# Wide matrix products as two half-width f32 products in place of three f32r products

## The chip, the cores and the metric

The kernel runs on one core of one Trainium2 chip. The metric is the device time of one execution in microseconds (us), lower is better. TensorE (PE) multiplies matrices, VectorE (DVE) and ScalarE (ACT) do elementwise work, GpSimd (POOL) a few odd jobs, and SyncE (SP) issues most transfers. PEld is TensorE's loading of the stationary operand, which the profile lists apart from the products (PE).

## The reference, cut to what matters

The reference is a two-layer decoder over 1024 tokens of width 1024 in float32. Each layer norms its input, projects it, mixes (pooling in layer 0, sliding-window attention in layer 1, and attention to 256 memory tokens in both), projects back, and then runs a squared-ReLU MLP of width 4096. All large products are float32 products:

```python
proj = rmsnorm(h, norm_mix[l]) @ w_in[l]
...
mkv = rmsnorm(mem, mem_norm[l]) @ w_mem_kv[l]
...
s = jnp.einsum('bshd,bmhd->bhsm', q, mk).astype(jnp.float32) * (HEAD_DIM ** -0.5)
...
h = h + jnp.concatenate([main_out, mem_out], axis=-1) @ w_out[l]
h = h + sq_relu_mlp(rmsnorm(h, norm_mlp[l]), w_up[l], w_down[l])
```

## The kernel before, in words

Features lie on the 128 partitions and tokens on the free axis, in two halves of 512. A wide product takes a stationary operand of 128x128 (weights) and a moving operand of 128x512 (activations) and adds into one PSUM bank. To keep float32 precision with the faster rounded type float32r, both operands are split: ACT writes a rounded copy, "hi", and DVE writes the remainder, "lo", which is the source minus hi. A product is then three float32r products, hi by hi, hi by lo, and lo by hi. This triple stands in four places of the code: `mm3` (lines 270 to 272; projections, memory keys, pooling, output projection of layer 1), `scores` (lines 515 to 517; attention scores), `Stream.run` (lines 938, 940 and 941; both MLPs and the output projection of layer 0, by a seven-product block scheme) and `plain_unit` (lines 1035 to 1037; the first step of each MLP). By the program, 2456 triples have 512 moving columns (1848 in `Stream.run`, 476 in `mm3`, 68 in `scores`, 64 in `plain_unit`) and 82 have 256.

Some other products are plain float32 already: transposes (`transpose4`, line 277, 128 columns), sums over heads or rows (lines 544, 313), and the attention's products with the values. These last have 64 output partitions each and come in twos, one for partitions 0 to 63 and one for 64 to 127: line 601 (128 columns, 128 products) in the memory attention, line 1484 (384 columns, 60 products) in the sliding window.

The splits are made in `split` (lines 233 to 237), `split_hi` and `split_lo` (lines 651 and 654), `stack_keys` (line 481) and a few places by hand. Weights come by DMA on SP's queue; the split MLP inputs are stored in DRAM once and fetched again for later blocks (`win`, 512 KB a transfer, hi and lo).

Order of the work: instructions of an engine run in the order in which they are written out. In the MLPs, `Stream` places each split, sum and eviction at a unit of four triples by due times and by the estimated load of DVE and ACT. In the attention stages, generators (`mem_attn`, `swa`, `head_stats`) are advanced by `tick(us)`, which is called with 0.65 after each triple; a generator's `yield 3.61` means that its next part is written out after triples worth 3.61 us. So the argument of `tick` sets how many wide products stand between two parts of the attention.

Of the kernel before, what the change touches and what calls it, by code (L numbers as in the profile page):

```python
# [10 lines left out]
F32R = mybir.dt.float32r  # L11
# [6 lines left out]
P = 128  # L18
# [23 lines left out]
def kernel(  # L42
# [25 lines left out]

# [44 lines left out]

    def x_tile(shape=None, dtype=F32R):
        return xp.tile(shape or [P, 2, HALF], dtype, tag="x", name="x")
# [113 lines left out]
    def split(src, dst, gain=None):  # L229

        hi, lo = dst[:, 0], dst[:, 1]
        if gain is None:
            nc.scalar.activation(hi, src, AF.Copy)
            nc.vector.tensor_tensor(lo, src, hi.bitcast(F32), op=ALU.subtract)  # L234
        else:
            nc.scalar.activation(hi, src, AF.Copy, scale=gain)
            nc.vector.scalar_tensor_tensor(lo, src, gain, hi.bitcast(F32), op0=ALU.mult, op1=ALU.subtract)
# [11 lines left out]
    def split_unit(raw, nk, gain=None):  # L249
        parts = []  # L250
        for k0 in range(0, nk, 4):
            n = min(4, nk - k0)
            r = raw[:, k0:k0 + n, :]
            if gain is not None:
                nc.gpsimd.tensor_tensor(  # L255
                    r, r, gain[:, k0:k0 + n].rearrange("p (k o) -> p k o", o=1).broadcast_to([P, n, P]), op=ALU.mult)
            w = wp.tile([P, 2, 4, P], F32R, tag="w", name="w")
# [6 lines left out]
    def mm3(ps, wsel, asel, ks, us=0.65):  # L264

        n = len(ks)
        for i, k in enumerate(ks):
            w0, w1 = wsel(k, 0), wsel(k, 1)
            a0, a1 = asel(k, 0), asel(k, 1)
# [71 lines left out]
    def load_x(nrm, between):  # L341
        for n in range(NK):
            h[n] = h_tile()
        xsum = small(NT, "xsum")
        toks = []
        load_gains()
        for t in range(NT):
            xt = g_tile()
            nc.sync.dma_start(out=xt, in_=x2[t * P:(t + 1) * P, :])
            toks.append(xt)  # L350
            if t == 1:
                between()
            if t == 7:
                load_vectors()
        def half(hf):
            tk = toks[4 * hf:4 * hf + 4]
            if hf == 0:
                banks = [tr_tile(), tr_tile(), mm_tile(), mm_tile(), mm_tile(), sps_tile(), sps_tile(), pv_tile().rearrange("p a t -> p (a t)")]
                for j in range(4):
                    for n in range(NK):  # L360
                        nc.tensor.transpose(banks[n][:, j * P:(j + 1) * P], tk[j][:, n * P:(n + 1) * P], ident)
            for n in range(NK):
                if hf == 0:
                    ps = banks[n]
# [10 lines left out]
                eng = nc.gpsimd if n % 3 == 1 else nc.vector  # L375
                eng.tensor_tensor(m[:, 1], h[n][:, hs(hf)], m[:, 0].bitcast(F32), op=ALU.subtract)
# [12 lines left out]
        return half, finish  # L389
# [29 lines left out]
    def mem_layer(l, alloc):  # L419
# [5 lines left out]
        for kk in range(4):  # L425
            m = alloc([P, 2, 2, MEMLEN], F32R)
# [37 lines left out]
        for u in range(4):  # L464
            wsel = load_unit([(ALL, w_mem_kv[l][:, u * P:(u + 1) * P])], NK)
            ps = mm_tile()[:, 0:MEMLEN]
            mm3(ps, wsel, asel, range(NK), 0.33)
# [7 lines left out]
    def stack_keys(src, hi, lo):  # L475


        for e in range(2):
            ln = slice(64 * e, 64 * e + 64)
            nc.scalar.activation(hi[e][ln], src[ln], AF.Copy)  # L480
            nc.vector.tensor_tensor(lo[e][ln], src[ln], hi[e][ln].bitcast(F32), op=ALU.subtract)

    def clear_other(t):

        for e in range(2):
            nc.gpsimd.memset(t[64 - 64 * e:P - 64 * e, :, e, :].bitcast(F32), 0.0)

    def mem_keys(kv):
        hi = z.mkp.tile([P, 2, 2, MEMLEN], F32R, tag="mkh", name="mkh")
        lo = z.mkp.tile([P, 2, 2, MEMLEN], F32R, tag="mkl", name="mkl")  # L490
        clear_other(hi)
        clear_other(lo)
        for j in range(2):
            stack_keys(kv[:, j * MEMLEN:(j + 1) * MEMLEN], [hi[:, j, e, :] for e in range(2)],
                       [lo[:, j, e, :] for e in range(2)])
        return hi, lo
# [3 lines left out]
    def query_stack(key, chunks, n):  # L500

        if n % 2 == 0:
            c = slice(n * P, n * P + 2 * P)
            out_ = []
            for q in chunks:
                st = z.qsp.tile([P, 2, 2 * P], F32R, tag="qs", name="qs")
# [5 lines left out]
    def scores(ps, st, n, khi, klo):  # L512
# [50 lines left out]
    def mem_attn(key, n, mk, vt, mq, rm, od):  # L563
# [4 lines left out]
        khi, klo = mk  # L568
# [3 lines left out]
        for j in range(2):  # L572
# [3 lines left out]
            scores(s_ps, qs[j], n, khi[:, j], klo[:, j])  # L576
# [76 lines left out]
    def split_lo(src, dst):  # L653
        nc.vector.tensor_tensor(dst[:, 1], src, dst[:, 0].bitcast(F32), op=ALU.subtract)  # L654
# [19 lines left out]
    class Stream:  # L674
# [16 lines left out]
        def stationary(self):  # L691

            turn[0] += 1
            return wp.tile([P, 2, 4, P], F32R, tag="w", name="w") if turn[0] % 5 else g_tile([P, 2, 4, P], F32R)
# [25 lines left out]
        def split_pieces(self, due, src, make, pre, x=0, w=0):  # L720
# [13 lines left out]
            b = self.piece(due, lambda: split_lo(src(), box[0]), dve=LO, pre=[a])  # L734
            return a, b, box

        def add_block(self, wt, b, fin, evac, pairs=range(4), cached=None, store=None, alloc=x_tile, b_in_x=False,
# [9 lines left out]
            for j, m in enumerate(ORDER):  # L747
# [7 lines left out]
                if cached:  # L755
                    for c in range(4):
                        def fetch(c=c, step=step, m=m):
                            t = step.win[c] = alloc([P, 2, HALF], F32R)
                            nc.sync.dma_start(out=t.bitcast(F32), in_=cached[m][c])
# [3 lines left out]
                else:  # L763
                    self.sums(m, b, fin, T, wins, first)
                    n, t = {1: (0, 0), 2: (1, 0), 3: (1, 1), 4: (0, 0), 5: (None, None), 6: (0, 0), 7: (0, 1)}[m]
                    for c in range(4):
# [8 lines left out]
                        def make(step=step, c=c):  # L775
                            step.win[c] = alloc([P, 2, HALF], F32R)
# [5 lines left out]
                        if store:  # L782
                            self.piece(first + 1, lambda m=m, c=c, step=step: nc.sync.dma_start(
                                out=store[m][c], in_=step.win[c].bitcast(F32)), pre=[lo], gap=1)
# [122 lines left out]
        def run(self, plain=()):  # L907
# [5 lines left out]
            for i in range(-len(plain), n):  # L913
# [22 lines left out]
                for k in range(4):  # L936
                    x_ = step.win[k]
                    nc.tensor.matmul(ps, w[:, 0, k, :], x_[:, 0], start=m in (1, 2, 7) and k == 0, stop=False,  # L938
                                     skip_group_check=True)
                    nc.tensor.matmul(ps, w[:, 0, k, :], x_[:, 1], start=False, stop=False, skip_group_check=True)  # L940
                    nc.tensor.matmul(ps, w[:, 1, k, :], x_[:, 0], start=False, stop=k == 3, skip_group_check=True)  # L941
                    tick(0.65)
# [40 lines left out]
    def mlp(l, nrm, gain, wt0, ws, hook, then=None):  # L983
        store = {m: [dr.tile([P, 2, HALF], F32, name=f"win{l}_{m}_{c}") for c in range(4)] for m in ORDER}
# [41 lines left out]
        def plain_unit(hf, q):  # L1026
            work = []
            for k in (2 * q, 2 * q + 1):
                for n in range(2):
                    def mm(k=k, n=n):  # L1030
# [4 lines left out]
                        nc.tensor.matmul(ps, w[:, 0, k % 4, :], x_[:, 0], start=k == 0, stop=False)  # L1035
                        nc.tensor.matmul(ps, w[:, 0, k % 4, :], x_[:, 1], start=False, stop=False)
                        nc.tensor.matmul(ps, w[:, 1, k % 4, :], x_[:, 0], start=False, stop=k == NK - 1)
# [164 lines left out]
    def pool_diff(c, hf, u, levels):  # L1202
# [16 lines left out]
        if (c, hf) == (1, 1):  # L1219
            d = z.dp.tile([P, 2, HALF], F32R, tag="d", name="d")  # L1220
        else:
            d = (g_tile if c else h_tile)([P, 2, HALF], F32R)
        d_t[hf][c] = d
        for (a, b, wi) in parts:
# [9 lines left out]
            nc.vector.tensor_tensor(d[a:b, 1], df[a:b, :], d[a:b, 0].bitcast(F32), op=ALU.subtract)  # L1234
# [115 lines left out]
    def head_unit(weights, gain, kgain, dst):  # L1350
# [3 lines left out]
        def tail(hf, ps):  # L1354
# [11 lines left out]
            else:  # L1366
                nc.vector.scalar_tensor_tensor(y, y, kgain, bp, op0=ALU.mult, op1=ALU.mult)
                yk = y.rearrange("p (b k) -> p b k", k=P)
                stack_keys(yk, [dst[hf][:, :, e, :] for e in range(2)], [dst[2 + hf][:, :, e, :] for e in range(2)])
# [29 lines left out]
    def k_unit(pr, alloc):  # L1399
        kh[pr] = [(alloc if i < 3 else g_tile)([P, 4, 2, P], F32R) for i in range(4)]  # L1400
# [15 lines left out]
    def swa(n, pr, put):  # L1416
# [15 lines left out]
        for i in range(3):  # L1432
# [3 lines left out]
            if first_ // 4 == last_ // 4:  # L1436
                kb = slice(first_ % 4, last_ % 4 + 1)
                scores(s_ps[:, 2 - nb:, :, :], qs[i], n, kh[pr][n // 4][:, kb], kh[pr][2 + n // 4][:, kb])
            else:
                for b, k in ((0, first_), (1, last_)):  # L1440
                    scores(s_ps[:, b, :, :], qs[i], n, kh[pr][k // 4][:, k % 4], kh[pr][2 + k // 4][:, k % 4])
# [160 lines left out]
```

## Time and profile before

| | |
|---|---|
| time, median of 2 runs | 1921.91 us (1920.87 to 1922.95) |
| profiled execution: time, span | 1920.99 us, 1919.3 us |
| granted TensorE clock, mean | 0.997 |
| PE busy | 1875.7 us (98%) |
| PEld busy | 1519.3 us (79%) |
| DVE busy | 1416.0 us (74%) |
| ACT busy | 985.9 us (51%) |

An engine's busy time is the time in which at least one of its instructions runs; products overlap in the records, so the distance from one start to the next is a product's price, not its own duration. A row of a timeline has the start and the length of a run of equal instructions and, in brackets, what ended the engine's idle time before it.

### The profile page before, as it was taken

To read this page: it belongs to the slowest core of one execution; us is meant where nothing else is said; L and a number is where in the kernel's file an instruction comes from. 1 tells how busy PE (TensorE), PEld (TensorE's weight loads), DVE (VectorE), ACT (ScalarE), POOL (GpSimd) and SP (SyncE) were. 2 spreads that over 40 slices of the span, in tenths; PEclk is the share of its full clock that TensorE was granted. 3 is DMA by queue.
4 is the path that set the end of the run, shared out by engine and by line. 5 is a ranking of instruction groups with operands and counts; after the bars stand their busy time and mean duration, and the time that the engine had idled before them with its cause. 6 is when DMAs were issued, how large, how long until landed. Compare 5 with 4: busy or idle time off the path is not lost. (4 is left out here: it accounts for less than half of the span.)

```text
span 1919.3 us, 24542 instructions
## 1 busy us (share of the span) xinstructions
PE 1875.7 (98%) x8786; PEld 1519.3 (79%) x8786; DVE 1416.0 (74%) x2577; ACT 985.9 (51%) x2063; POOL 197.4 (10%) x244
## 2 busy tenths in 40 slices
PE   8999999999999999999999999999999999999999
PEld 6867878878888888888768776787888888888887
DVE  6788899896496497489673668679885596496495
ACT  7553654843553553555453666555643643543553
POOL 4502120000000000001424221140000000000000
PEclk9999999999999999999999999999999999999999
DMA  6311423617307407411211123234546227307412
GB/s 253 110 28 52 175 78 142 263 70 278 135 23 285 154 24 262 175 55 67 88 39 39 28 73 97 62 104 197 198 161 226 96 90 262 132 24 284 153 45 66
DMA packets 139052, 244.44 MB, mean 127 GB/s; under 512 B 20852, under 2 KB 67762, under 8 KB 138930
## 3 DMA queue, kind: packets, MB, share of 16 engines
q1 hardware_dynamic: 137458, 238.15, 35.6%
q10 hardware_dynamic: 1472, 4.73, 0.6%
q8 instruction: 69, 1.13, 0.2%
q14 instruction: 53, 0.43, 0.1%
HBM read 196.71 MB, written 46.14 MB: 127 GB/s over the span
## 5 line engine op out<-in xcount | busy, mean ns | idle before, releaser
L651 ACT ACTIVATE w<-wa 128x512 fp32r<-128x512 f32 x371 | 230.9, 624 | 216.4 <-PE mm L941 99.5
L654 DVE TENSOR_TENSOR w<-wa,w 128x512 fp32r<-128x512 f32 x371 | 255.2, 688 | 100.0 <-ACT w L651 99.9
L941 PE MATMUL mm<-x,w 128*128 128x512 f32 x676 | 263.4, 390 | 1.1 <-DVE w L654 1.1
L938 PE MATMUL mm<-x,w 128*128 128x512 f32 x676 | 263.5, 390 | 0.2 <-DVE h L974 0.2
L940 PE MATMUL mm<-x,w 128*128 128x512 f32 x676 | 263.1, 389 | 0.0
L270 PE MATMUL mm<-x,w 128*128 128x512 f32 x448 | 183.4, 411 | 3.9 <-DVE h L374 2.1
L938 PE MATMUL sps<-x,w 128*128 128x512 f32 x468 | 182.8, 391 | 2.3 <-ACT x L651 2.3
L966 DVE TENSOR_TENSOR wa<-wa 128x512 f32<-128x512 f32 x264 | 181.0, 693 | 5.3 <-DMA wa<-in_w_up 4.6
L941 PE MATMUL sps<-x,w 128*128 128x512 f32 x468 | 182.5, 390 | 1.0 <-DVE w L654 1.0
L940 PE MATMUL sps<-x,w 128*128 128x512 f32 x468 | 182.1, 389 | 0.0
L272 PE MATMUL mm<-x,w 128*128 128x512 f32 x448 | 178.0, 398 | 1.0 <-DVE w L234 0.9
L271 PE MATMUL mm<-x,w 128*128 128x512 f32 x448 | 178.4, 399 | 0.4 <-DVE x L234 0.4
L941 PEld LDWEIGHTS mm<-x,w 128*128 128x128 f32 x676 | 126.9, 188 | 28.7 <-DVE w L654 2.2
L938 PEld LDWEIGHTS mm<-x,w 128*128 128x128 f32 x676 | 126.9, 188 | 26.8 <-issue 0.6
L940 PEld LDWEIGHTS mm<-x,w 128*128 128x128 f32 x676 | 126.9, 188 | 26.3
L651 ACT ACTIVATE x<-g 128x512 fp32r<-128x512 f32 x192 | 115.4, 620 | 54.9 <-DVE g L966 54.9
L654 DVE TENSOR_TENSOR x<-g,x 128x512 fp32r<-128x512 f32 x192 | 132.1, 688 | 9.1 <-ACT x L651 9.1
L974 DVE TENSOR_TENSOR h<-mm,h 128x512 f32<-128x512 f32 x124 | 85.0, 685 | 38.4 <-PE mm L941 38.4
L255 POOL TENSOR_TENSOR raw<-raw,cols 128x512 f32<-128x512 f32 x40 | 47.1, 1197 | 639.5 <-DMA raw<-in_w_in 597.5
L997 ACT ACTIVATE g<-g 128x512 f32<-128x512 f32 x90 | 56.9, 632 | 103.9 <-DVE g L1016 103.9
L270 PEld LDWEIGHTS mm<-x,w 128*128 128x128 f32 x448 | 85.0, 190 | 26.2 <-issue 5.3
L938 PEld LDWEIGHTS sps<-x,w 128*128 128x128 f32 x468 | 87.9, 188 | 21.4 <-ACT x L651 3.1
(353 smaller groups left out, 4035.5 us busy)
## 6 DMA issues: line engine op xcount, KB each, us to landing
x<-win SPq DMA_DIRECT2D x168, 512.0 KB, 6.1
wa<-in_w_up SPq DMA_DIRECT2D x32, 1024.0 KB, 5.8
wa<-in_w_down SPq DMA_DIRECT2D x32, 1024.0 KB, 5.1
win<-x SPq DMA_DIRECT2D x56, 512.0 KB, 3.0
h<-hd SPq DMA_DIRECT2D x16, 512.0 KB, 3.6
raw<-in_w_in SPq DMA_DIRECT2D x10, 512.0 KB, 3.8
g<-in_x SPq DMA_DIRECT2D x8, 512.0 KB, 6.7
raw<-in_w_mem_kv SPq DMA_DIRECT2D x8, 512.0 KB, 3.7
```

What stands on the lines that cost most here:

```text
L255: nc.gpsimd.tensor_tensor(r, r, gain[:, k0:k0 + n].rearrange("p (k o) -> p k o", o=1).broadcast_to([P, n, P]), op=ALU.mult)
L270: nc.tensor.matmul(ps, w0, a0, start=i == 0, stop=False)
L271: nc.tensor.matmul(ps, w0, a1, start=False, stop=False)
L272: nc.tensor.matmul(ps, w1, a0, start=False, stop=i == n - 1)
L651: nc.scalar.activation(dst[:, 0], src, AF.Copy)
L654: nc.vector.tensor_tensor(dst[:, 1], src, dst[:, 0].bitcast(F32), op=ALU.subtract)
L938: nc.tensor.matmul(ps, w[:, 0, k, :], x_[:, 0], start=m in (1, 2, 7) and k == 0, stop=False, skip_group_check=True)
L940: nc.tensor.matmul(ps, w[:, 0, k, :], x_[:, 1], start=False, stop=False, skip_group_check=True)
L941: nc.tensor.matmul(ps, w[:, 1, k, :], x_[:, 0], start=False, stop=k == 3, skip_group_check=True)
L966: eng.tensor_tensor(out_, a, b, op=op)
L974: nc.vector.tensor_tensor(c, ps, c, op=ALU.add)
L997: nc.scalar.activation(c, c if src is None else src, AF.Relu)
```

## The change

Operands stay float32: hi is a plain float32 copy that ACT makes, and no remainder is made. A wide product is two plain float32 products with the same moving operand, one of stationary columns 0 to 63 into PSUM partitions 0 to 63, one of columns 64 to 127 into partitions 64 to 127. `tick` gets 0.43 in place of 0.65 (0.22 in place of 0.33 at 256 columns). Operand tiles and the `win` transfers have half the bytes.

```diff
 def split(src, dst, gain=None):
-        hi, lo = dst[:, 0], dst[:, 1]
         if gain is None:
-            nc.scalar.activation(hi, src, AF.Copy)
-            nc.vector.tensor_tensor(lo, src, hi.bitcast(F32), op=ALU.subtract)
+            nc.scalar.activation(dst[:, 0], src, AF.Copy)
...
-    def mm3(ps, wsel, asel, ks, us=0.65):
+    def pair(ps, w, a, start, stop, **kw):
+        for e in (slice(0, 64), slice(64, P)):
+            nc.tensor.matmul(ps[e], w[:, e], a, start=start, stop=stop, **kw)
+
+    def mm3(ps, wsel, asel, ks, us=0.43):
...
-            nc.tensor.matmul(ps, w0, a0, start=i == 0, stop=False)
-            nc.tensor.matmul(ps, w0, a1, start=False, stop=False)
-            nc.tensor.matmul(ps, w1, a0, start=False, stop=i == n - 1)
+            w0, a0 = wsel(k, 0), asel(k, 0)
+            pair(ps, w0, a0, i == 0, i == n - 1)
             tick(us)
...
     def scores(ps, st, n, khi):
-        nc.tensor.matmul(ps, st[:, 0, t], khi, start=True, stop=False)
-        nc.tensor.matmul(ps, st[:, 0, t], klo, start=False, stop=False)
-        nc.tensor.matmul(ps, st[:, 1, t], khi, start=False, stop=True)
+        pair(ps, st[:, 0, t], khi, True, True)
...
     def split_lo(src, dst):
-        nc.vector.tensor_tensor(dst[:, 1], src, dst[:, 0].bitcast(F32), op=ALU.subtract)
+        pass
...
             for k in range(4):
                     x_ = step.win[k]
-                    nc.tensor.matmul(ps, w[:, 0, k, :], x_[:, 0], start=m in (1, 2, 7) and k == 0, stop=False,
-                                     skip_group_check=True)
-                    nc.tensor.matmul(ps, w[:, 0, k, :], x_[:, 1], start=False, stop=False, skip_group_check=True)
-                    nc.tensor.matmul(ps, w[:, 1, k, :], x_[:, 0], start=False, stop=k == 3, skip_group_check=True)
-                    tick(0.65)
+                    pair(ps, w[:, 0, k, :], x_[:, 0], m in (1, 2, 7) and k == 0, k == 3, skip_group_check=True)
+                    tick(0.43)
```

PE's order in the memory attention of layer 0, before: transposes of the weights `s`, products with the values (`pv<-pt,mkv`) and wide products of the projection (`mm<-x,w`) alternate.

```order
L277 MATMUL tr<-ident,s 128x128 x8
L270 MATMUL mm<-x,w 128x512
L271 MATMUL mm<-x,w 128x512
L272 MATMUL mm<-x,w 128x512
...
L601 MATMUL pv<-pt,mkv 64x128
L271 MATMUL mm<-x,w 128x512
L277 MATMUL tr<-ident,s 128x128 x4
L601 MATMUL pv<-pt,mkv 64x128 x3
```

The same place after the change (line 261 is the product in `pair`, 273 the transpose, 587 the product with the values):

```order
L273 MATMUL tr<-ident,s 128x128 x8
L261 MATMUL mm<-x,w 64x512 x4
L273 MATMUL tr<-ident,s 128x128 x4
L261 MATMUL mm<-x,w 64x512
L273 MATMUL tr<-ident,s 128x128 x4
L261 MATMUL mm<-x,w 64x512
L587 MATMUL pv<-pt,mkv 64x128 x8
```

The products with the values now stand together, wide products of 64 output partitions stand alone between transposes of 128, and a pair can be cut in two by them. Over the whole program PE's order goes from half-width to full-width products and back 113 times, 59 times before.

DVE's order in the first MLP, before (lines 654 are the remainders, 966 sums, 974 evictions):

```order
L654 TENSOR_TENSOR x<-g,x 128x512
L654 TENSOR_TENSOR w<-wa,w 128x512
L966 TENSOR_TENSOR wa<-wa 128x4x128
L974 TENSOR_TENSOR h<-sps,h 128x512
L654 TENSOR_TENSOR w<-wa,w 128x512
L654 TENSOR_TENSOR x<-g,x 128x512
```

After the change (sums are line 949, evictions 957):

```order
L949 TENSOR_TENSOR wa<-wa 128x4x128
L949 TENSOR_TENSOR g<-g 128x1024
L957 TENSOR_TENSOR h<-pv,h 128x512
L949 TENSOR_TENSOR wa<-wa 128x4x128
L957 TENSOR_TENSOR h<-sps,h 128x512
```

The remainders are gone from DVE's order and nothing takes their place there.

## Rows read from the trace of the kernel before

**Rows 1.** The page: span, busy time of the engines, granted clock in 40 slices.
```profile
span 1919.3 us, 24542 instructions
PE 1875.7 (98%) x8786; PEld 1519.3 (79%) x8786; DVE 1416.0 (74%) x2577; ACT 985.9 (51%) x2063; POOL 197.4 (10%) x244
PEclk9999999999999999999999999999999999999999
```

**Rows 2.** What PE waited for: total us, times, longest; longest in total first.
```profile
PE mm L361 <- POOL t L163: 4.3, 1, 4.3
PE sps L515 <- ACT s L582: 3.8, 4, 1.5
PE tr L277 <- DVE t L1360: 2.4, 2, 1.8
...
PE mm L361 <- DMA g<-in_x: 0.4, 1, 0.4
```

**Rows 3.** Line 940, window 500 to 800 us: duration min/median/max, first and last start.
```profile
L940 PE MATMUL mm<-x,w x179: 389/389/389, 500.0 to 792.4; 128*128 128x512 f32 x179
L940 PE MATMUL sps<-x,w x116: 389/389/389, 504.8 to 797.9; 128*128 128x512 f32 x116
L940 PE MATMUL pv<-x,w x59: 389/389/389, 510.2 to 799.9; 128*128 128x512 f32 x59
L940 PE MATMUL mm<-x,g x40: 389/389/389, 502.1 to 776.1; 128*128 128x512 f32 x40
L940 PE MATMUL sps<-x,g x32: 389/389/389, 556.5 to 762.5; 128*128 128x512 f32 x32
L940 PE MATMUL pv<-x,g x16: 389/389/389, 570.1 to 789.7; 128*128 128x512 f32 x16
```

**Rows 4.** PE's timeline, triples of 512 columns beside the attention.
```profile
1143.09 0.39 PE L271 MATMUL mm<-x,w 128*128 128x512 f32 x1
1143.32 0.40 PE L272 MATMUL mm<-x,w 128*128 128x512 f32 x1
1143.55 0.40 PE L270 MATMUL mm<-x,w 128*128 128x512 f32 x1
...
1144.01 0.40 PE L272 MATMUL mm<-x,w 128*128 128x512 f32 x1
```

**Rows 5.** PE's timeline, a triple of 256 columns in the memory layer.
```profile
54.01 0.28 PE L271 MATMUL mm<-g,w 128*128 128x256 f32 x1
...
54.37 0.28 PE L271 MATMUL mm<-g,w 128*128 128x256 f32 x1
```

**Rows 6.** Line 1484: all records of its products and loads on one of its tiles.
```profile
L1484 PEld LDWEIGHTS pv<-pt,g x88: 132/137/137, 1074.2 to 1245.3; 128*64 128x64 f32 x88
L1484 PE MATMUL pv<-pt,g x88: 486/486/537, 1074.5 to 1245.6; 128*64 128x384 f32 x88
L1484 PE MATMUL pv<-pt,h x32: 486/512/537, 1073.8 to 1152.9; 128*64 128x384 f32 x32
```

**Rows 7.** PE's timeline, two products of line 1484, then two more.
```profile
1152.57 0.87 PE L1484 MATMUL pv<-pt,h 128*64 128x384 f32 x4
1153.26 0.81 PE L1484 MATMUL pv<-pt,g 128*64 128x384 f32 x4
```

**Rows 8.** PE's timeline, line 1484 alone and in twos, between full-width products.
```profile
1175.66 0.27 PE L277 MATMUL tr<-ident,s 128*128 128x128 f32 x1
1175.86 0.86 PE L1484 MATMUL pv<-pt,g 128*64 128x384 f32 x2
1176.65 0.50 PE L270 MATMUL mm<-x,w 128*128 128x512 f32 x1
1177.08 0.87 PE L1484 MATMUL pv<-pt,g 128*64 128x384 f32 x4
```

**Rows 9.** Line 601: all its records (as rows 6), then eight products on PE's timeline.
```profile
L601 PE MATMUL pv<-pt,mkv x256: 272/273/324, 97.6 to 1014.8; 128*64 128x128 f32 x128
...
1011.53 1.09 PE L601 MATMUL pv<-pt,mkv 128*64 128x128 f32 x16
```

**Rows 10.** PEld's timeline, the loads for the products of rows 7.
```profile
1152.57 0.20 PEld L1484 LDWEIGHTS pv<-pt,h 128*64 128x64 f32 x4
1152.94 0.14 PEld L1484 LDWEIGHTS pv<-pt,g 128*64 128x64 f32 x2 [0.18 <-issue]
```

**Rows 11.** The page: the largest remainder groups on DVE, the rounded copies on ACT.
```profile
L651 ACT ACTIVATE w<-wa 128x512 fp32r<-128x512 f32 x371 | 230.9, 624 | 216.4 <-PE mm L941 99.5
L654 DVE TENSOR_TENSOR w<-wa,w 128x512 fp32r<-128x512 f32 x371 | 255.2, 688 | 100.0 <-ACT w L651 99.9
L654 DVE TENSOR_TENSOR x<-g,x 128x512 fp32r<-128x512 f32 x192 | 132.1, 688 | 9.1 <-ACT x L651 9.1
```

**Rows 12.** The page: the largest group of transfers, KB each and us to landing.
```profile
x<-win SPq DMA_DIRECT2D x168, 512.0 KB, 6.1
```

More of the change, by code (lines that the diff above doesn't have):

```diff
@@ L112, in g_tile, with x_tile @@
         return gp.tile(shape or [P, S], dtype, tag="g", name="g")
-    def x_tile(shape=None, dtype=F32R):
-        return xp.tile(shape or [P, 2, HALF], dtype, tag="x", name="x")
+    def x_tile(shape=None, dtype=F32):
+        return xp.tile(shape or [P, 1, HALF], dtype, tag="x", name="x")
     def t_tile(shape=None):
@@ L229, in split @@
     def split(src, dst, gain=None):
-        hi, lo = dst[:, 0], dst[:, 1]
         if gain is None:
-            nc.scalar.activation(hi, src, AF.Copy)
-            nc.vector.tensor_tensor(lo, src, hi.bitcast(F32), op=ALU.subtract)
-        else:
-            nc.scalar.activation(hi, src, AF.Copy, scale=gain)
-            nc.vector.scalar_tensor_tensor(lo, src, gain, hi.bitcast(F32), op0=ALU.mult, op1=ALU.subtract)
+            nc.scalar.activation(dst[:, 0], src, AF.Copy)
+        else:
+            nc.scalar.activation(dst[:, 0], src, AF.Copy, scale=gain)
     def fetch_unit(srcs, nk):
@@ L425, in mem_layer @@
         for kk in range(4):
-            m = alloc([P, 2, 2, MEMLEN], F32R)
+            m = alloc([P, 1, 2, MEMLEN], F32)
             for i in range(2):
@@ L466, in mem_layer @@
             ps = mm_tile()[:, 0:MEMLEN]
-            mm3(ps, wsel, asel, range(NK), 0.33)
+            mm3(ps, wsel, asel, range(NK), 0.22)
             y = y_tile([P, MEMLEN])
@@ L473, in mem_layer, with stack_keys @@
         return kv, vt
-    def stack_keys(src, hi, lo):
+    def stack_keys(src, hi):
         for e in range(2):
@@ L480, in stack_keys @@
             nc.scalar.activation(hi[e][ln], src[ln], AF.Copy)
-            nc.vector.tensor_tensor(lo[e][ln], src[ln], hi[e][ln].bitcast(F32), op=ALU.subtract)
     def clear_other(t):
         for e in range(2):
-            nc.gpsimd.memset(t[64 - 64 * e:P - 64 * e, :, e, :].bitcast(F32), 0.0)
+            nc.gpsimd.memset(t[64 - 64 * e:P - 64 * e, :, e, :], 0.0)
     def mem_keys(kv):
-        hi = z.mkp.tile([P, 2, 2, MEMLEN], F32R, tag="mkh", name="mkh")
-        lo = z.mkp.tile([P, 2, 2, MEMLEN], F32R, tag="mkl", name="mkl")
+        hi = z.mkp.tile([P, 2, 2, MEMLEN], F32, tag="mkh", name="mkh")
         clear_other(hi)
-        clear_other(lo)
         for j in range(2):
-            stack_keys(kv[:, j * MEMLEN:(j + 1) * MEMLEN], [hi[:, j, e, :] for e in range(2)],
-                       [lo[:, j, e, :] for e in range(2)])
-        return hi, lo
+            stack_keys(kv[:, j * MEMLEN:(j + 1) * MEMLEN], [hi[:, j, e, :] for e in range(2)])
+        return hi
     stacks = {}
@@ L505, in query_stack @@
             for q in chunks:
[L506 removed]
+                st = z.qsp.tile([P, 1, 2 * P], F32, tag="qs", name="qs")
                 split(q[:, c], st)
@@ L575, in mem_attn @@
             s_ps = sps.tile([P, 2, 256], F32, tag="sps", name="sps")
-            scores(s_ps, qs[j], n, khi[:, j], klo[:, j])
+            scores(s_ps, qs[j], n, mk[:, j])
             m = small(2, "mm2")
@@ L757, in fetch @@
                         def fetch(c=c, step=step, m=m):
-                            t = step.win[c] = alloc([P, 2, HALF], F32R)
-                            nc.sync.dma_start(out=t.bitcast(F32), in_=cached[m][c])
+                            t = step.win[c] = alloc([P, 1, HALF], F32)
+                            nc.sync.dma_start(out=t, in_=cached[m][c])
                         pre = [self.last_x] if self.last_x else []
@@ L775, in make @@
                         def make(step=step, c=c):
-                            step.win[c] = alloc([P, 2, HALF], F32R)
+                            step.win[c] = alloc([P, 1, HALF], F32)
                             return step.win[c]
@@ L783, in add_block @@
                             self.piece(first + 1, lambda m=m, c=c, step=step: nc.sync.dma_start(
-                                out=store[m][c], in_=step.win[c].bitcast(F32)), pre=[lo], gap=1)
+                                out=store[m][c], in_=step.win[c]), pre=[lo], gap=1)
                     if b_in_x:
@@ L937, in run @@
                     x_ = step.win[k]
-                    nc.tensor.matmul(ps, w[:, 0, k, :], x_[:, 0], start=m in (1, 2, 7) and k == 0, stop=False,
-                                     skip_group_check=True)
-                    nc.tensor.matmul(ps, w[:, 0, k, :], x_[:, 1], start=False, stop=False, skip_group_check=True)
-                    nc.tensor.matmul(ps, w[:, 1, k, :], x_[:, 0], start=False, stop=k == 3, skip_group_check=True)
-                    tick(0.65)
+                    pair(ps, w[:, 0, k, :], x_[:, 0], m in (1, 2, 7) and k == 0, k == 3, skip_group_check=True)
+                    tick(0.43)
                 if self.then and step is self.steps[-1] and p in (step.pairs[0], step.pairs[-1]):
@@ L983, in mlp @@
     def mlp(l, nrm, gain, wt0, ws, hook, then=None):
-        store = {m: [dr.tile([P, 2, HALF], F32, name=f"win{l}_{m}_{c}") for c in range(4)] for m in ORDER}
+        store = {m: [dr.tile([P, 1, HALF], F32, name=f"win{l}_{m}_{c}") for c in range(4)] for m in ORDER}
         st = Stream(w_live=2)
@@ L1034, in mm @@
                         x_, w, ps = xs[hf][k], ws[n, k // 4], banks[hf, n][1]
-                        nc.tensor.matmul(ps, w[:, 0, k % 4, :], x_[:, 0], start=k == 0, stop=False)
-                        nc.tensor.matmul(ps, w[:, 0, k % 4, :], x_[:, 1], start=False, stop=False)
-                        nc.tensor.matmul(ps, w[:, 1, k % 4, :], x_[:, 0], start=False, stop=k == NK - 1)
+                        pair(ps, w[:, 0, k % 4, :], x_[:, 0], k == 0, k == NK - 1)
                     work.append(mm)
@@ L1219, in pool_diff @@
         if (c, hf) == (1, 1):
-            d = z.dp.tile([P, 2, HALF], F32R, tag="d", name="d")
+            d = z.dp.tile([P, 1, HALF], F32, tag="d", name="d")
         else:
-            d = (g_tile if c else h_tile)([P, 2, HALF], F32R)
+            d = (g_tile if c else h_tile)([P, 1, HALF], F32)
         d_t[hf][c] = d
@@ L1368, in tail @@
                 yk = y.rearrange("p (b k) -> p b k", k=P)
-                stack_keys(yk, [dst[hf][:, :, e, :] for e in range(2)], [dst[2 + hf][:, :, e, :] for e in range(2)])
+                stack_keys(yk, [dst[hf][:, :, e, :] for e in range(2)])
         for hf in range(2):
@@ L1399, in k_unit @@
     def k_unit(pr, alloc):
-        kh[pr] = [(alloc if i < 3 else g_tile)([P, 4, 2, P], F32R) for i in range(4)]
+        kh[pr] = [alloc([P, 4, 2, P], F32) for i in range(2)]
         for t in kh[pr]:
```

19 lines of the change are left out of this document (6 added, 13 removed).

## The prediction, on record before the changed kernel ran

> **What bounds the kernel now.** I read the page first. PE is busy for 1875.7 of 1919.3 us, the granted clock is full in every slice (the upper of its two levels, 2.4 GHz), and DVE and ACT have a quarter and half of the span free [rows 1]. Then the waits of PE: the longest sum is 4.3 us, at the start, and transfers cost it 0.4 us [rows 2]. So PE is the bound almost everywhere, and the time is the sum of what its products take in succession. What DVE, ACT or the queues save can win back only part of the 43.6 us in which PE is idle. The question is therefore one number: does a pair of half-width f32 products take PE less time than three f32r products?
>
> **What a triple costs now.** In the quiet stretch of the first MLP, 500 to 800 us, line 940 has 179+116+59+40+32+16 = 442 records, one a triple, so a triple takes 300/442 = 0.679 us, or 0.226 us a product [rows 3]. The 0.389 us that a record lasts is more, since records overlap. Beside the attention, starts lie 0.23 us apart (0.92 us over four), a triple 0.69 [rows 4]. With 1848+64 triples of the first kind and 476+68 of the second, the mean is 0.682 us. At 256 columns, starts lie 0.12 us apart (0.36 over three), so a triple is 0.36 us [rows 5].
>
> **What a pair will cost.** The trace has this very form in another size: line 1484 multiplies plain f32 with 64 output partitions and 384 columns, in twos for the lower and the upper half.
>
> - A product has two records. The program has 60 such products, and there are 88+32 = 120 records [rows 6]. I call each record a pass.
> - Two products of different halves run at the same time. One product alone takes 0.86 us, two together 0.87 us [rows 8].
> - How long a pass takes in succession: the second group of rows 7 starts at 1153.26 and lasts 0.81 us; its last record is 0.486 us long [rows 6, 7], so its second pass starts 0.81 - 0.486 = 0.32 us after the first. The first distance after a full-width product is some 0.06 us longer (0.87 - 0.486 = 0.38 [rows 6, 7]). At 128 columns, eight products in twos, sixteen records, make eight passes in 1.09 us, of which the last record takes 0.27 and the longer first distance 0.06: (1.09 - 0.27 - 0.06)/7 = 0.11 us a pass [rows 9].
> - Both are close to 0.84 us per 1000 columns, two cycles of the granted 2.4 GHz a column (0.833 ns) and some 2.5 ns more. For 512 columns a pass is then 0.429 us, a pair of two passes 0.858 us, and at 256 columns 0.432 us.
>
> So a wide product of 512 columns goes from 0.682 to 0.858 us. Two instructions in place of three look cheaper, but each of the two is two passes at half the column rate: 4 x 512 column-cycles in place of 3 x 512, plus less overhead per load.
>
> **The sum**, against the profiled span of 1919.3 us:
>
> - Pairs of 512: 2456 x (0.858 - 0.682) = **+432 us**. Lower bound 2456 x 2 x 0.427 (no overhead at all) gives +422; if each pass had the 13 ns over 0.213 us that an f32r product shows in rows 3, 0.440 a pass, +486.
> - Pairs of 256: 82 x (0.432 - 0.36) = +6 us.
> - Changes between full and half width. A product of half width after a transpose ends its first record later than in succession: transpose end 1175.93, first record end 1175.86 + 0.54 = 1176.40, 0.47 us against 0.32, so 0.15. On the way back 1176.72 to 1177.15 [rows 8], 0.43 against 0.23, so up to 0.20, and to a transpose, which is the common case now, I take 0.15. The order has 113 such excursions in place of 59: 54 x 0.3 = +16 us. Bounds: 0, and 54 x 0.35 = +19.
> - Cut pairs: a half product that stands alone takes as long as a pair [rows 8]. Of the 113 runs of half-width products 24 have an odd number: 24 x 0.43 = +10 us. Lower bound 0, upper 20 where neighbours have unequal lengths.
> - Remainders leave DVE (255.2 + 132.1 us in the two largest groups alone [rows 11]) and POOL clears fewer keys. On PE's path this is worth nothing where PE is busy, as it nearly always is. It shortens the waits before splits and attention parts, and PE's longer products give ACT and DVE more time between them. `tick` moves the same way: 0.43 is called for 0.858 us of work, so a `yield` of 3.61 now stands for eight or nine pairs, some 7 us, where it was six triples, 4 us. Of the 39 us of idle after the first product (43.6 less the 4.3 of the start [rows 2]) I take 15 back; bounds 0 and 30. ACT's copies stay as they are in number and size [rows 11].
> - `win` transfers halve [rows 12]; PE waits for transfers 0.4 us in all [rows 2], so this is 0. SP's order does not change at the places that PE waits for.
>
> Sum: 1919.3 + 432 + 6 + 16 + 10 - 15 = 2368 us of span. The profiled execution took 1.7 us more than its span, and lies 0.9 us under the median of the runs. I round to a forecast of **2369 us**, 23% slower.
>
> **A rule against the rows.** The loads for the second pair start at 1152.94 [rows 10], while the first pair's products run until 1153.44 [rows 7], and all four loads of the first pair are over within 0.20 us; the next products start without a gap for them. The Trainium skill, "TensorE: Matmul & The Clock Gate", Part 3 (The mechanism), says that loading the stationary operand overlaps running products only when their row groups differ, and both halves here use all rows; the rows contradict that rule for this form. It is rival B.
>
> **The rivals.**
>
> - **A. One pass a product at half rate, faster.** If the second record of a product were only the other half of the output or an artefact of two different moving operands, a pair with one shared moving operand would take 0.429 us: 2456 x (0.429 - 0.682) = -621, some 1310 us, with PE still above ACT's 986 us [rows 1]. The place is every wide pair; it decides once a pair is under 0.682 us. For it: the change gives `tick` 0.43 a pair. Against it: a product that is alone, with no second stream, has its two records at the same distance as two together [rows 8]. The Trainium skill, "Perfetto Trace Analysis", Engine Utilization, gives the array's rate for the low-high f32 form as half of full; read as the price of a whole product it leads to this rival, and the rows say that it holds for each of the two passes. Chance 0.03.
> - **B. Loads not hidden, slower still.** Each pass would wait for a load of 0.137 us [rows 6], both halves at once: pair 0.858 + 0.274 = 1.132 us, 2456 x 0.45 = +1105, some 3040 us. It does not happen in [rows 7, 10]. Chance 0.02.
> - **C. The halves fall out of step** in a stream of nearly 1800 pairs, where [rows 7, 9] show two and four in succession. If they never overlapped, a pair would be 1.717 us and the time some 4480 us; part of that, a tenth of the pairs, would be +210 us, 2580 us. Against it: the sixteen records of [rows 9] keep step. Chance 0.04.
>
> The forecast keeps 0.91. Within it, the lower bounds together (422 for the pairs, no cut pairs, 30 won back) give 2335 us and the upper ones (486, 19, 20, nothing won back) 2452. They will hardly all fall together, so the range is 2330 to 2440, and it leaves out A, B, C and a little at the upper side. Faster by over 2%: 0.03 (A). Within 2%, which is about what a measurement of this kernel can tell: 0.01. Slower: 0.96.
>
> **What would show it.** In the changed profile, starts of line 261's records in the MLP lie in twos, 0.01 us apart (0.87 against 0.86 in rows 8), and 0.43 us from one two to the next; PE stays at 98% or above, DVE falls by more than the 387 us of the two groups of rows 11, and ACT stays near 986 us. If the distance is 0.213 us, A is right; 0.57 us, B; single records 0.43 us apart, C. The forecast is wrong if half-width products at 512 columns do not scale from 128 and 384, or if the attention's stretches (920 to 1260 us now) gain far more idle than the -15 us says.

## The result, and the profile after

The changed kernel takes 2353.8 us (median; 2353.5 to 2354.09), the kernel before 1921.91 us (1920.87 to 1922.95): a ratio of 1.2247, 95% interval 1.2195 to 1.23. The forecast was 2369 us, slower, with a range of 2330 to 2440. Of the kernel of experiment e1 one execution, the profiled one, took 5843.87 us, with its passes 0.89 to 1.24 us apart at a granted clock of 1.00, for a reason that stays open; it is left out of the comparisons, and its trace is not read below.

The page of the changed kernel, first its span, busy times and granted clock, then the groups that answer to [rows 11] and [rows 12]:

```profile
span 2352.3 us, 28640 instructions
PE 2326.8 (99%) x11324; PEld 847.8 (36%) x11324; DVE 797.9 (34%) x1495; ACT 989.6 (42%) x2063; POOL 168.8 (7%) x226
PEclk9999999999999999999999999999999999999999
...
L637 ACT ACTIVATE w<-wa 128x512 f32<-128x512 f32 x371 | 230.5, 623 | 452.0 <-PE mm L261 198.2
...
x<-win SPq DMA_DIRECT2D x168, 256.0 KB, 2.9
```

Against [rows 1], DVE lost 618 of its 1416 us and ACT gained 4; PE went from 98% to 99% busy, with 90% or more of the full clock in every slice of 59 us (a digit 9). Everything the change saves was saved on an engine that was not the bound. The remainder groups that [rows 11] show on DVE are gone, and the copies on ACT are the same 371 as before.

What PE pays is read in the quiet stretch of the first MLP. These are the product records of line 261 (the product in `pair`) between 500 and 800 us: duration min/median/max in ns, first and last start; the shape at the end is counted in a sample where its number is smaller. They answer to [rows 3].

```profile
L261 PE MATMUL mm<-x,w x552: 592/592/593, 499.8 to 799.8; 128*64 128x512 f32 x184
...
L261 PE MATMUL sps<-x,w x352: 592/592/593, 524.3 to 795.1; 128*64 128x512 f32 x176
...
L261 PE MATMUL pv<-x,w x208: 592/592/593, 507.1 to 784.8; 128*64 128x512 f32 x104
...
L261 PE MATMUL mm<-x,g x144: 592/592/593, 572.3 to 747.0; 128*64 128x512 f32 x144
...
L261 PE MATMUL sps<-x,g x112: 592/592/593, 503.7 to 781.4; 128*64 128x512 f32 x112
...
L261 PE MATMUL pv<-x,g x32: 592/592/592, 692.5 to 798.5; 128*64 128x512 f32 x32
```

The counts add up to 1400 records. Two passes of two halves are four records, so this is 350 pairs in 300 us, 0.857 us each; the triples made 442 in the same 300 us. Two windows of PE's timeline that begin at the same record (start, us, what) give the distance directly:

```profile
599.81 0.60 PE L261 MATMUL mm<-x,w 128*64 128x512 f32 x2
...
599.81 4.46 PE L261 MATMUL mm<-x,w 128*64 128x512 f32 x20
```

Two records together last 0.60 us, so they run side by side, and every further two add 0.43 us: (4.46 - 0.60)/9 = 0.429. The loads lie under them, and the products follow each other without a gap; PEld's records in the same place (start, us, what):

```profile
600.24 0.14 PEld L261 LDWEIGHTS mm<-x,w 128*64 128x64 f32 x2 [0.28 <-issue]
600.67 0.14 PEld L261 LDWEIGHTS mm<-x,w 128*64 128x64 f32 x2 [0.28 <-issue]
```

One thing is new and was not forecast. What PE waited for (total us, times, longest), to be put beside [rows 2]:

```profile
PE mm L261 <- ACT w L637: 7.0, 1, 7.0
PE mm L357 <- DMA g<-in_x: 4.6, 1, 4.6
PE tr L273 <- DVE s L1441: 3.6, 2, 2.3
PE mm L261 <- DVE h L370: 2.1, 1, 2.1
```

The first line is a single wait of 7.0 us at 239 us, where PE wants ACT's first copy of the `w_out` weights. ACT is only the last link. (The last number of a row is the longest single wait.) The chain of waits between 220 and 250 us (start, us, what) names the others:

```profile
219.98 18.05 PE mm L261 x84
...
238.05 7.15 DMA wa<-in_w_out
...
245.22 0.64 ACT w L637
...
245.90 4.37 PE mm L261 x11
```

The transfer of those weights is issued at 238.05 us, and its 7.15 us lie open. SP's queue shows why it is so late, after the change and then before it:

```profile
204.07 33.44 SPq L1087 DMA_DIRECT2D h<-hd  x7
238.05 0.38 SPq L626 DMA_DIRECT2D wa<-in_w_out  x1
```

```profile
190.60 0.38 SPq L640 DMA_DIRECT2D wa<-in_w_out  x1
191.08 3.19 SPq L1106 DMA_DIRECT2D h<-hd  x6
```

Before, the first transfer of `wa` stood ahead of the reloads of `h`; now it stands behind seven of them, which take until 237.5 us and themselves wait, 19.6 us of it for PE's products and 9.9 for a copy on ACT. What it was issued on shows in the products that read tile `d`:

```profile
L261 PE MATMUL mm<-d,w x12: 592/592/592, 229.3 to 237.4; 128*64 128x512 f32 x12
```

The last of them ends at 237.4 + 0.59 = 238.0, and at 238.05 the transfer goes out. Experiment e5 tests whether it is `d` that holds it.

The wait costs more than its 7.0 us. Two stretches, one ahead of it and one right behind it (window, its length, busy us and instructions of each engine, granted clock, DMA share, GB/s):

```profile
230.00:238.00 8.00, 8.00 (x40) 2.73 (x38) 1.87 (x3) 2.75 (x4) 0.00 (x0) 1.00 0.00 0
245.80:249.00 3.20, 3.10 (x8) 1.01 (x10) 0.00 (x0) 1.61 (x4) 0.00 (x0) 0.50 1.05 404
```

Behind the wait, in which PE did nothing, the granted clock is 0.50, the lower of its two levels, and the passes that start at 245.90, 246.81, 247.66 and 248.52 us are 0.85 to 0.91 us apart in place of 0.43: 1.3 us more. From 249 to 252 us it is at 0.98 again. The page's slices are too long to show it.

### The profile page after: what moved, and what is told of

It reads as the page before. It is cut to its first block, busy times and chain, and to the rows that moved or that the text cites. A ratio compares the mean times of both kernels' runs of the same rounds, so it can differ in the third digit from the quotient of the medians.

```text
span 2352.3 us, 28640 instructions
## 1 busy us (share of the span) xinstructions
PE 2326.8 (99%) x11324; PEld 847.8 (36%) x11324; DVE 797.9 (34%) x1495; ACT 989.6 (42%) x2063; POOL 168.8 (7%) x226
## 4 chain that ended last, share of the span: by engine, by line
PE 97%; ACT 1%; DVE 1%; DMA 1%; issue 0%; SPq 0%; ACTq 0%
PE mm L261 54%; PE sps L261 26%; PE pv L261 12%; PE tr L273 2%; PE tr L531 1%; PE pv L1464 1%; PE pv L587 1%; PE tr L309 0%; DMA wa<-in_w_out 0%; ACT s L1431 0%; DMA g<-in_x 0%; ACT s L568 0%; ACT qs L230 0%; ACT x L230 0%; DVE g L1195 0%
## 5 line engine op out<-in xcount | busy, mean ns | idle before, releaser
L261 PE MATMUL mm<-x,w 128*64 128x512 f32 x4640 | 1071.8, 595 | 3.3 <-DVE h L370 2.1
L261 PEld LDWEIGHTS mm<-x,w 128*64 128x64 f32 x4640 | 338.1, 137 | 627.9 <-issue 607.6
L261 PE MATMUL sps<-x,w 128*64 128x512 f32 x1920 | 429.5, 592 | 0.0
L637 ACT ACTIVATE w<-wa 128x512 f32<-128x512 f32 x371 | 230.5, 623 | 452.0 <-PE mm L261 198.2
L261 PEld LDWEIGHTS sps<-x,w 128*64 128x64 f32 x1920 | 137.6, 137 | 272.5 <-issue 268.8
L261 PE MATMUL pv<-x,w 128*64 128x512 f32 x976 | 220.2, 592 | 0.0
L261 PE MATMUL mm<-x,g 128*64 128x512 f32 x736 | 167.3, 592 | 0.0
L637 ACT ACTIVATE x<-g 128x512 f32<-128x512 f32 x192 | 114.3, 614 | 0.9 <-PE mm L261 0.9
L261 PE MATMUL sps<-x,g 128*64 128x512 f32 x480 | 109.0, 592 | 0.0
L261 PE MATMUL mm<-g,w 128*64 128x512 f32 (+1 forms) x564 | 100.9, 504 | 7.0 <-ACT w L637 7.0
```

Source lines behind the costliest of these rows:

```text
L261: nc.tensor.matmul(ps[e], w[:, e], a, start=start, stop=stop, **kw)
L637: nc.scalar.activation(dst[:, 0], src, AF.Copy)
```

## The experiments

**e1, full width.** The pair becomes one f32 product of 128 output partitions.

```diff
-        for e in (slice(0, 64), slice(64, P)):
-            nc.tensor.matmul(ps[e], w[:, e], a, start=start, stop=stop, **kw)
+        nc.tensor.matmul(ps, w, a, start=start, stop=stop, **kw)
```

> One plain f32 product of 128 output partitions in place of each pair. Theory (a plain f32 product is two passes at half the column rate, whatever its width, so a pair costs what one full-width product costs): pass distance 0.43 us, and the 113 changes of width and the cut pairs are gone, some 33 and 10 to 20 us, so 2300 to 2320 us. Rival (the halving is what makes f32 affordable, a full-width f32 product costs as much as two halves in succession): 1.7 us a product, some 4400 us. Second rival (loading 128 stationary columns is not hidden at two loads a product): 0.1 to 0.2 us a pass more, 2800 to 3300 us.

Measured: 2323.5 to 2325.1 us, ratio 1.2081 (1.2061 to 1.2101). That is 3 to 5 us above the expected range, which took all 113 changes of width for gone; by the trace of e7, 36 stay, since the attention's products with the values remain at half width. Plain f32 at full width is 29 us faster than in halves by the medians, 32 by the ratios (1.2247 - 1.2081, times 1922); the chips differ by that little, and where two numbers stand below they are these two. Cutting the output in two buys nothing; why, its twin e7 shows in a trace.

**e2, lower half.** All lower-half products remain; of the upper half only the first product of each group is issued, so the rest of it is left out.

```diff
-        for e in (slice(0, 64), slice(64, P)):
-            nc.tensor.matmul(ps[e], w[:, e], a, start=start, stop=stop, **kw)
+        nc.tensor.matmul(ps[0:64], w[:, 0:64], a, start=start, stop=stop, **kw)
+        if start:
+            nc.tensor.matmul(ps[64:P], w[:, 64:P], a, start=True, stop=True, **kw)
```

> Of each accumulation group only the first product is made for the upper half; the rest of the upper half's products is left out, the lower half is whole. Theory (the halves run at the same time): a lower product alone still takes 0.858 us, so 2335 to 2356 us, the same as the change within 1%. Rival (the halves take turns on PE): about half of the wide products' time goes, 1300 to 1500 us.

Measured: 2340.47 us, ratio 1.2165 (1.214 to 1.2189). Two stretches of its timeline:

```profile
602.24 3.60 PE L260 MATMUL mm<-x,g 128*64 128x512 f32 x8
605.67 0.59 PE L260 MATMUL sps<-x,w 128*64 128x512 f32 x1
```

Eight single records take 3.60 us, so their distance is (3.60 - 0.59)/7 = 0.43 us, the same as that of twos in the change. Most of the upper half's work was free: with it gone the time falls by only 13 to 16 us. So the halves do run at once, and what sets the time is the columns streamed for one of them.

**e3, triples without remainders.** The products of before, three rounded ones each, but all three of the rounded operand itself; no remainder is made. The two mixed products are left out of the result in this way. Cut to its core (tiles go back to the rounded type, `tick` to 0.65):

```diff
-        for e in (slice(0, 64), slice(64, P)):
-            nc.tensor.matmul(ps[e], w[:, e], a, start=start, stop=stop, **kw)
+        for i in range(3):
+            nc.tensor.matmul(ps, w, a, start=start and i == 0, stop=stop and i == 2, **kw)
```

> The kernel before without its remainders: three f32r products of 128 output partitions from the rounded copies alone (hi by hi three times), no remainder made or loaded; this leaves the two mixed products' values out. PE's work is that of before, DVE's that of the change. Theory (DVE was off PE's path): 15 us of waits come back at most, 1900 to 1920 us. Rival (the remainders were on the path in many places): 1850 us or less.

Measured: 1902.63 us, ratio 0.9891 (0.9876 to 0.9906). Its page, and its longest wait on PE's timeline with the products behind it:

```profile
PE 1864.5 (98%) x8786; PEld 1521.2 (80%) x8786; DVE 792.5 (42%) x1495; ACT 984.9 (52%) x2063; POOL 170.4 (9%) x226
...
207.42 8.87 PE L262 MATMUL mm<-g,w 128*128 128x512 f32 x27 [8.64 <-ACT w L638]
```

DVE lost 624 us, about as much as in the change, and the kernel gained 1.1%. So this is what the omission of the remainders is worth with triples: 21 us net, more than the 15 us that were expected at most. A wait of 8.6 us for the `w_out` copy came in here too, and the 27 products behind it take 8.87 us where 26 x 0.226 + 0.39 = 6.3 us would do; without both it would be some 32 us, an estimate (21 + 8.6 + 2.6) that no run tests. The other half of the change, the pairs, costs the rest.

**e4, remainders back.** The change, with every remainder made again in f32 (and not used), tiles, `win` transfers and the load that `Stream` books on DVE for remainders back at their old size. The line that does most of it:

```diff
-        pass
+        nc.vector.tensor_tensor(dst[:, 1], src, dst[:, 0].bitcast(F32), op=ALU.subtract)
```

> The change with the remainders made again (plain f32, never multiplied) and the win transfers at 512 KB again, PE's pairs as they are. Theory (PE's path alone counts): 2350 to 2365 us. Rival (removing the remainders won back much of what the pairs lost): 2400 us or more.

Measured: 2356.14 us, ratio 1.2242 (1.2222 to 1.2263), 2.3 us over the change by the medians, 1 us under it by the ratios. The page and the largest group on DVE:

```profile
PE 2331.3 (99%) x11324; PEld 849.4 (36%) x11324; DVE 1427.7 (61%) x2577; ACT 991.8 (42%) x2063; POOL 189.9 (8%) x244
...
L654 DVE TENSOR_TENSOR w<-wa,w 128x512 f32<-128x512 f32 x371 | 255.2, 688 | 157.6 <-ACT w L651 157.4
```

630 us more on DVE, with as good as no effect. But the 7.0 us wait is not among its waits, with tiles of the old size. Set against e5, which lacks it as well, the remainders, with the sizes that came back with them, cost 10 to 13 us.

**e5, d apart.** The change, with tile `d` (the products' operand just ahead of the wait) in a pool of its own, open for the whole program, so that its memory isn't given to the first `wa` buffer.

```diff
+    dp = pool("dp", 1)
...
-            d = z.dp.tile([P, 1, HALF], F32, tag="d", name="d")
+            d = dp.tile([P, 1, HALF], F32, tag="d", name="d")
```

> The change with the tile d of the last pooled block in a pool of its own, so that the first load of w_out needs no memory that pooling still reads and stands ahead of the reloads of h on SP's queue again. Theory (the 7.0 us wait of PE at 239 us comes from that place in the memory and the queue): 5 to 8 us less than the change, 2346 to 2349 us. Rival (the load waits for transfers or for other buffers anyway): 2352 us or more.

Measured: 2343.13 us, ratio 1.2188 (1.2171 to 1.2204), 11 us less than the change (10.7 by medians, 11.3 by ratios), more than a wait of 7.0 us and more than the 5 to 8 us expected. SP's queue, then PE's longest waits:

```profile
215.84 0.38 SPq L627 DMA_DIRECT2D wa<-in_w_out  x1
216.32 3.07 SPq L1088 DMA_DIRECT2D h<-hd  x6
```

```profile
PE mm L358 <- DMA g<-in_x: 4.6, 1, 4.6
PE tr L274 <- DVE s L1442: 3.6, 2, 2.3
```

The transfer stands ahead of the reloads again, 22 us earlier, and the wait is gone. So the place of the buffers is the cause: in the change the first `wa` buffer fell on memory that was still being read, and the transfer had to stand behind that reader. That the reader is `d`, and no neighbour that moved together with it, goes by the times above (238.0 and 238.05). That smaller tiles packed the pools otherwise is what e4 adds, where the old sizes go without the wait. Taken record by record, the products of the two kernels drift apart by 7.2 us at the wait, by 1.3 us in the passes at the lower clock behind it, by 0.7 us by 1406 us, and by 1.3 us more at 1512 to 1516 us, where the clock fell once more in the change and not in e5, after a wait of 2.3 us that both have. The last two steps are not traced to `d`.

**e6, tick 0.65.** The change, with the work that `tick` hands out counted as before (0.65 and 0.33 a pair in place of 0.43 and 0.22).

```diff
-    def mm3(ps, wsel, asel, ks, us=0.43):
+    def mm3(ps, wsel, asel, ks, us=0.65):
...
-                        tick(0.43)
+                        tick(0.65)
```

> The change with tick at 0.65 (0.33) as before, so that the parts of the attention stand closer together among the pairs. Theory (the larger distance in PE time, 0.43 for 0.858 us of work, is what took the attention's waits away): waits of PE come back and 16 more changes of width cost 0.3 us each, 5 to 20 us more than the change, 2359 to 2374 us. Rival (the pairs' length alone covers the attention's parts): 2350 to 2358 us.

Measured: 2363.88 us, ratio 1.2291 (1.2274 to 1.2308), 8 to 10 us slower than the change. Its longest waits:

```profile
PE mm L261 <- ACT w L637: 8.0, 1, 8.0
...
PE tr L273 <- DVE t L1340: 4.3, 6, 1.8
PE mm L261 <- ACT h L368: 2.8, 1, 2.8
```

The last two are not among the five longest of the change, but others are shorter: by the count that the last part makes of the idle term, waits cost 29.5 us here and 28.3 in the change. So that waits come back with closer spacing, as the theory has it, is not shown. What the order shows is 129 excursions to half width in place of 113: 16 x 0.3 = 5 us of the 8 to 10. The rest is not placed.

**e7, full width, d apart.** e1 and e5 together.

> Full-width f32 products as in the first experiment, with d apart. Theory: 5 to 8 us less than the 2325 us of the full-width products, 2316 to 2320 us; pass distance 0.43 us (0.427 and 2 to 10 ns). Rival: the full-width pass is longer than the half-width one by over 10 ns, which would eat what the saved changes of width give.

Measured: 2314.07 us, ratio 1.2034 (1.2018 to 1.205), 2 us under the expected range and again 29 us less than the same in halves (e5, 2343.13). Its timeline, and the longest run of loads in 500 to 800 us:

```profile
2230.67 0.60 PE L273 MATMUL tr<-ident,h 128*128 128x128 f32 x4
2231.11 1.02 PE L261 MATMUL sps<-x,g 128*128 128x512 f32 x2
2231.97 2.74 PE L261 MATMUL sps<-x,w 128*128 128x512 f32 x6
2234.54 0.60 PE L273 MATMUL tr<-ident,h 128*128 128x128 f32 x4
...
L261 PEld LDWEIGHTS sps<-x,w x184: 190/190/190, 502.1 to 790.1; 128*128 128x128 f32 x184
```

Six records take 2.74 us: (2.74 - 0.592)/5 = 0.43 us a pass, as in halves. The loads take 0.190 us each instead of twice 0.137, and stay hidden as well. The same place of the change:

```profile
2267.03 0.66 PE L273 MATMUL tr<-ident,h 128*128 128x128 f32 x4
2267.61 1.08 PE L261 MATMUL sps<-x,g 128*64 128x512 f32 x4
2268.52 2.74 PE L261 MATMUL sps<-x,w 128*64 128x512 f32 x12
2271.20 0.66 PE L273 MATMUL tr<-ident,h 128*128 128x128 f32 x4
```

From one group of transposes to the next the change needs 2271.20 - 2267.03 = 4.17 us, the full width 2234.54 - 2230.67 = 3.87 us, for the same work. The 0.30 us is one excursion to half width and back, as forecast. Of this, 0.14 lies before the first half product (0.58 against 0.44 us after the transposes' start) and 0.16 behind the last.

**e8, one rounded product.** One full-width product of the rounded operands for each wide product; the two mixed products are left out, so the values are coarser than the reference's.

```diff
-        for e in (slice(0, 64), slice(64, P)):
-            nc.tensor.matmul(ps[e], w[:, e], a, start=start, stop=stop, **kw)
+        nc.tensor.matmul(ps, w, a, start=start, stop=stop, **kw)
```

(with the operands' tiles in the rounded type)

> One f32r product of 128 output partitions in place of each pair, from the rounded copy; the two mixed products are left out, so the values are coarser. Theory (the time follows PE's price of a wide product until another engine binds): 2456 x 0.227 + 82 x 0.12 in place of 2107 + 35, so PE alone would need some 800 us; ACT is busy for 990 us, so 1000 to 1200 us with ACT as the bound. Rival (DVE, transfers or the attention's chains hold the kernel far above): 1400 us or more.

Measured: 1240.4 us, ratio 0.6451 (0.6435 to 0.6466), above the expected 1000 to 1200. Page, waits, and four products ahead of and behind one such wait on PE's timeline:

```profile
PE 920.9 (74%) x3710; PEld 655.0 (53%) x3710; DVE 778.3 (63%) x1495; ACT 937.0 (76%) x2063; POOL 171.5 (14%) x226
...
PEclk9777878778797788787879897988787798788779
...
PE mm L261 <- ACT w L637: 50.4, 42, 9.7
PE mm L261 <- DVE h L957: 48.1, 13, 7.3
...
404.22 1.07 PE L261 MATMUL mm<-x,g 128*128 128x512 f32 x4
...
414.79 2.05 PE L261 MATMUL sps<-x,w 128*128 128x512 f32 x4 [7.69 <-DVE h L957]
```

Here PE is no longer the bound. ACT is now a little busier than PE (76% against 74%), and PE waits for its copies and for DVE's evictions. The granted clock averages 0.837, stretches at the lower level among those at the upper: it is 1.00 from 400 to 406 us and 0.50 from 414 to 424 us, behind the wait of 7.7 us, where four products take 2.05 us in place of 1.07. Here DVE's and ACT's work counts; in neither of the two kernels compared is PE's work short enough for that.

**e9 and e10, before with another tick.** The kernel before with 0.43 and 0.22, and with 0.52 and 0.26, in place of 0.65 and 0.33.

```diff
-    def mm3(ps, wsel, asel, ks, us=0.65):
+    def mm3(ps, wsel, asel, ks, us=0.43):
```

> The kernel before, three f32r products and remainders, with tick at 0.43 (0.22) in place of 0.65 (0.33), nothing else. Theory (the distance of the attention's parts in PE time is worth something by itself: at 0.65 in the change it cost 10 us): 5 to 20 us less than before, 1902 to 1917 us. Rival (the spacing only helps beside pairs; before, the waits come from DVE's remainders): 1918 to 1930 us.

> The same with tick at 0.52 (0.26). Theory: between before and the tick of 0.43, 1908 to 1920 us. Rival: no difference, or slower where a wait moves, 1920 to 1930 us.

Measured: 1929.99 us, ratio 1.0038 (1.0025 to 1.0052), and 1925.97 us, ratio 1.0012 (1.0003 to 1.002). The rival held both times: what helps the pairs does not help the triples. The longest wait of e9:

```profile
PE tr L277 <- DVE s L1461: 5.6, 2, 5.4
```

A wait of 5.4 us for the memory attention's weights `s` came in, longer than any in [rows 2]. No version here beats the kernel before with the same products formed; e3 and e8 are faster by what they leave out.

## Why the prediction was right, point by point

- **The pair's price, +432 us, held.** 0.858 us forecast, 0.857 measured over 350 pairs. The scaling from products of 384 and 128 columns to 512 was sound, since a pass costs two cycles a column (2 x 512 / 2.4 GHz = 0.427 us) and some 2 ns (0.429 measured). e3 beside the change puts a number on pairs alone: without remainders either way, triples 1902.6 and pairs 2353.8 us, 451 us apart, where the pairs with their width changes and cuts were forecast at 432 + 6 + 16 + 10 = 464. By the count below, e3 also loses 12 us more to waits than the change (40.6 against 28.3 us), about the difference.
- **Rival A fell.** A product has two passes of 0.429 us. The half rate that the Trainium skill, "Perfetto Trace Analysis", Engine Utilization, gives for the low-high f32 form agrees with one pass (0.429 us against the 0.213 of 512 columns at one a cycle), not with a whole product; that plain f32 here is that form is taken from the rate alone.
- **Rival B fell.** The rule of the Trainium skill, "TensorE: Matmul & The Clock Gate", Part 3 (The mechanism), that loads overlap products only when their row groups differ, is contradicted here in both forms: loads of 0.137 us for 64 columns and of 0.190 us for 128, all with every row in use, cost PE no time. The same section also lets a load into the background weight buffer go ahead of running products, which is not at odds with them.
- **Rival C fell.** From 500 to 800 us all 1400 starts lie in twos, and e2 with mostly one half has the same distance.
- **Width changes and cut pairs, +16 and +10, held in price; their sum is not measured alone.** One excursion costs 0.30 us where it can be seen alone. Full width is 29 us faster (e1, and e7 against e5 on one chip), but that saves 113 - 36 = 77 excursions, not 54: 77 x 0.30 = 23 us, and some 8 for odd runs (24 against 6, these of 384 columns), 31 in all. What the forecast left out is that the order of before has cut twos too: 38 of its 59 runs of half-width products have an odd number (30 of 128 columns, 8 of 384), by the same reckoning 30 x 0.11 + 8 x 0.32 = 6 us that the change saves.
- **The idle term, -15, was too small.** Without it the sum is 2383 us; the span is 2352.3, 31 us less. Take over all of PE's records the distance from one record's end to the next, and count by how much it exceeds the usual one of its form and the form before it (where by over 0.1 us; passes at the lower clock count too). By this count waits cost 56.2 us in 106 places before and 28.3 us in 59 after: 28 us won back, though a new wait of 7.0 us was added. The forecast took its stock from the page's idle (39 us after the first product) and so missed what records longer than their slots hide: 0.389 against 0.226 us before, 0.16 us for each wait. With -28 in place of -15 the sum is 1919.3 + 432 + 6 + 26 - 28 = 2355 us, and 2349 with the 6 us for the cut twos of before; the span lies between, 3 us from either. Why the waits shrank is shown in part: with the remainders made again (e4, which has no wait of 7 us) they cost 29.0 us, 27 less than before, so most of the saving does not come from the remainders' omission, which is worth 11 more (18.1 us in e5). That it comes from PE's longer products is left by elimination; no run tests it alone.
- **One step failed: "SP's order does not change at the places that PE waits for."** It was priced at 0 and cost a wait of 7.0 us, 8.5 with the slow passes behind it (the drift of the records in e5), and 11 in the time (e5), because buffers now lay on memory that was still being read. It did not show in the total, since the idle term was too small by more than that.
- **That the remainders are worth little held.** 10 to 13 us beside pairs (e4 against e5), 21 us beside triples (e3; some 32 by the estimate there), of 618 us of DVE time.
- **Two sums of the forecast are a little off.** Its lower end of 2335 us keeps the full +16 for changes of width, whose lower bound it gives as 0; with that it is 2319. And 2368 us of span with the 1.7 and 0.9 us that it names is 2371, not 2369. With either, 2354 lies in the range.

## What to carry to other kernels

Count a change of TensorE's number format in cycles a column, from records of that form at another size in the same trace, never in instructions: the two f32 halves side by side are two passes of two cycles, four in place of the three of the rounded products. Two halves that stream the same operand side by side take the time of one full product, so they save nothing and pay 0.30 us for every excursion to half width and back. And when tiles shrink or grow, read the order of the queue that loads the next stage's buffers anew: a pool that is packed otherwise can set a transfer behind a reader that it never had.

## What the runs showed of the hardware that was not expected

- A plain f32 product at full width has the same 0.429 us a pass as one of 64 output partitions, and its loads of 0.190 us are hidden as well (e7). Nothing in the trace of before had this form at 512 columns.
- Where PE waits often (e8, 74% busy), its granted clock averaged 0.837 over the span, and behind a wait of 7.7 us four products took 2.05 us in place of 1.07. In the change, 99% busy, the page shows 90% or more of the full clock in every slice, and still a single wait of 7.0 us was followed by 3 us at the lower level, which cost 1.3 us more.
